# The first norm of a hybrid encoder block: loads, weight halves, scaling and two weight sums moved to other engines

## The chip, the core and the metric

The kernel runs on one core of a Trainium2 chip. The core has a matrix engine (TensorE, PE in the profile), a vector engine (VectorE, DVE), an activation engine (ScalarE, ACT), a general engine (GpSimd, POOL) and a sequencer that asks for transfers (SyncE, SP). Each runs its own list of instructions in order and waits on semaphores where it needs what another engine or a DMA has made. The metric is the device time of one execution in microseconds.

## The reference

Inputs are float32. The hidden state is 16 meta tokens followed by x, 1024 tokens of 1024 channels.

```python
def rmsnorm(x, g):
    y = xf * lax.rsqrt(jnp.mean(xf * xf, axis=-1, keepdims=True) + EPS)
    return (y * g).astype(x.dtype)

h = concat([meta, x])
u = rmsnorm(h, norm_mix)
z = u @ w_in                     # 4112 columns: a, q, k, v, r, lr, ga, gb
p = multiscale_pool(a)           # trailing means of 2, 4, 8, 16 tokens, minus the token
o = gla_chunked(q, k, v, log_sigmoid(lr @ w_gate_up + b_gate) / 16)
m = sigmoid(ga) * (p-branch) + sigmoid(gb) * (o-branch)
h = h + m @ w_out
h = h + square(relu(rmsnorm(h, norm_ffn) @ w_ff1)) @ w_ff2
out = rmsnorm(h, norm_final)[16:]
```

## The kernel before

Every matrix product is computed as three products of split operands (a high part, rounded to the matrix engine's fast 32-bit type, and a low part, the rest): high x high, low x high, high x low. ACT makes the high part, DVE subtracts it from the value to make the low part. After the norm come the gate, q and r columns of `w_in` (the class `Quarters`: a Strassen-like scheme of seven products P1 to P7 over pairs of weight blocks, each block first split into high and low), the pooling branch, the linear attention, the merge, and the MLP. The change touches the function `start`, which is the first 45 us or so, and what `Quarters` makes ready in it.

What `start` does:

- It asks for x's first tile of 128 tokens (`load(0)`, into the buffer `xs` of four tiles), the identity matrix, the norm weight (`g8`, in the first rows of the tile `xm`), x's second tile, two raw tiles of v weights (`fetch_vw`), and x's third and fourth tile, all on SP, in this order; POOL asks for the sixteen `lr` columns. The two raw tiles hold the v columns 0 to 127 and 128 to 255, each for all 1024 input rows.
- For each tile t of 128 tokens: `squared` (ACT squares it and sums each row), `root` (two small ACT instructions), `rest` (the inverse root, refined with three to five tiny instructions; on DVE for tiles 0 to 2, on POOL from tile 3 on, and for the meta tokens, tile 8), `normed` (DVE multiplies the tile by its inverse root into `us`, L664, SP then asks for tile t + 4, and PE transposes the result into two PSUM banks, L582), `taken` (DVE multiplies the transposed halves by the norm weight into `ut`, L589; ACT makes the high half `th`, L598; DVE the low half `tl`, L599).
- `warm(n)` lets PE transpose the identity into a bank that nobody reads, 4, 8 and 12 times (`WARM`), between the first real steps.
- `load_vw` splits the v weights: `hi` on ACT (L475), `lo` on DVE (L478), `lr` for the sixteen more columns. `v_tile` is the product of one tile of tokens with these 272 columns, eight k steps for each of the three parts. Tiles 0 and 1 run part by part ("hh", "lh", "hl", L510), tiles 2 to 7 step by step (L256 to L258). Two PSUM banks take them in turn, and ACT evacuates each into `v` (L525) and `lrtok` (L529).
- In the last turns of the loop `q.prime` splits the first weight blocks of `Quarters`. Its P5 operand is the sum of two halves of a weight block; DVE adds them (L325) into a half of the tile `fs`. `differences` then makes sums and differences of the `ut` quarters, on DVE, and steps through the first products (`next(run)`).

The order of the work around the change is written by hand: in `start` ACT, DVE and POOL run in program order (`manual_schedule`), and PE does so everywhere. SP's list follows the calls, and an SP request waits until the buffer that it fills is read out, with all later requests behind it.

```python
for t in range(1, 8):
    left_now, leave = leave, v_tile(0, t, True)   # t > 1
    if t < 6: b[t + 2] = normed(t + 2)
    for fn in left_now: fn()                      # evacuate tile t - 1
    if t < 6: rest(t + 3)
    lows = list(taken(b[t + 1], t + 1))
    if t < 5: squared(t + 4); root(t + 4)
    for fn in lows: fn()
    for n in {5: (0,), 6: (1, 2), 7: (3,)}.get(t, ()): q.prime(n == 0)
```

Of the kernel before, what the change touches and what calls it, by code (L numbers as in the profile page):

```python
# [33 lines left out]
WARM = (4, 8, 12)  # L34
# [80 lines left out]
def kernel(  # L115
# [173 lines left out]
    class Quarters:  # L289
# [4 lines left out]
        def __init__(self, n, block, places, result):  # L294
            self.n, self.block, self.places, self.result = n, block, places, result
            self.w, self.x, self.room = {}, {}, False
            self.leaving, self.lead = None, 0

        def load(self, i, u):
            dst = self.places[i % 2][u]  # L300
            self.w[i, u] = dst.rearrange("p (k c) -> p k c", k=KT)
            nc.sync.dma_start(self.w[i, u], self.block(2 * i + u))

# [11 lines left out]
        def sums(self):  # L315

            for p, i in self.order():
                a11, a12 = (self.w[i, 0][:, k : k + 4] for k in (0, 4))
                if p in ("P1", "P2"):
                    s = a11 if p == "P1" else a12  # L320
                else:
                    a21, a22 = (self.w[i, 1][:, k : k + 4] for k in (0, 4))
                    s = quad(S["fs"][:, i % 2] if p != "P7" else S["s3"])
                    if p == "P5":
                        dve.tensor_tensor(s, a21, a22, ALU.add)  # L325
                    elif p == "P6":
                        dve.tensor_tensor(s, s, a11, ALU.subtract)
                    elif p == "P7":
                        dve.tensor_tensor(s, a11, a21, ALU.subtract)
                    elif p == "P3":  # L330
                        dve.tensor_tensor(s, a12, s, ALU.subtract)
                    elif p == "P4":
                        s = a22
                yield p, i, s
# [132 lines left out]
    def fetch_vw(i):  # L467
        return [raw.load(w_cols(C_V + i * 256 + j * P), D).rearrange("p (k c) -> p k c", k=KT) for j in range(2)]

    def load_vw(i, raws=None, parts=False):  # L470
        vw, raws = S["vw"][i], raws or fetch_vw(i)
        c = [slice(j * P, (j + 1) * P) for j in range(2)]

        def hi(j):
            act.activation(vw[:, 0, :, c[j]], raws[j], ACT.Copy)  # L475

        def lo(j):
            dve.tensor_tensor(vw[:, 1, :, c[j]], raws[j], f32(vw[:, 0, :, c[j]]), ALU.subtract)  # L478
# [14 lines left out]
    def v_tile(i, t, later=False, by_part=False, by_k=False):  # L493
# [12 lines left out]
        def part(name):  # L506
            left_of["n"] -= 1
            l, r = parts[name]
            for k in range(KT):
                pe.matmul(b, l[:, k], r[:, k], start=name == "hh" and k == 0, stop=left_of["n"] == 0 and k == KT - 1)  # L510
# [115 lines left out]
    def start():  # L626
        act.preload_act_table_set("natural_log_exp_and_others")
# [22 lines left out]
        load(0)  # L650
        nc.sync.dma_start(ident, ident_in)
        nc.sync.dma_start(g8, norm_mix.rearrange("(k p) -> k p", p=P))
        load(1)
# [7 lines left out]
        def normed(t):  # L661

            x_, u = of(t)
            dve.tensor_scalar(u, x_, rs[t], None, ALU.mult)  # L664
# [3 lines left out]

        def warm(n):

            for _ in range(n):
                pe.transpose(idle[:, :P], ident, ident)
# [4 lines left out]
        with tc.manual_schedule(engines={mybir.EngineType.Activation, mybir.EngineType.DVE, mybir.EngineType.Pool}):  # L677
# [15 lines left out]
            warm(WARM[1])  # L693
            squared(0)
# [6 lines left out]
            lows = [list(taken(b[0], 0))]  # L701
            rest(1)
            warm(WARM[2])
            b[1] = normed(1)
            hi, lo, lr = load_vw(0, raws, True)
            hi(0)
            hi(1)
            lr_lo = lr()
            v0, leave0 = v_tile(0, 0, by_part=True)
            v1, leave = v_tile(0, 1, by_part=True)  # L710
            v0("hh")
# [3 lines left out]
            lows.append(list(taken(b[1], 1)))  # L715
            v1("hh")
            for j in range(2):
                lo(j)
            lr_lo()
# [15 lines left out]
            for t in range(1, 8):  # L735
# [17 lines left out]
                if t < 6:  # L753
                    rest(t + 3)
                lows = list(taken(b[t + 1], t + 1)) if t < 7 else []
# [1097 lines left out]
```

## Time and profile before

| what | value |
|---|---|
| three executions | 1212.27, 1213.29 and 4245.53 us; median 1213.29 |
| the profiled execution | 1212.85 us, of which the span from first to last instruction is 1211.0 |
| PE, DVE, ACT, POOL busy | 98%, 72%, 51%, 5% of the span |
| mean granted TensorE clock | 0.998 |
| bytes moved | 182 MB, mean 150 GB/s |

The profile shows one execution. Its rows give the start of an instruction or of a group in microseconds from the start of the span, its length, the engine, the line of the kernel, the operation and out<-in by the names of the tiles, and in brackets how long the engine had been idle before it and what ended that. Lengths of neighbours on an engine overlap a little, so the distance between two starts is the better price of a step in a sequence. A matmul row's end is modelled; a PE that shows no gap is taken as busy.

### The profile page before, as it was taken

Reading aid. Unit: us, or ns where it says so; the run is one execution under the profiler, and the core shown is the slowest. Engines: PE = TensorE matmul, PEld = TensorE weight load, DVE = VectorE, ACT = ScalarE, POOL = GpSimd, SP = SyncE. Lnnn points to the kernel's source line nnn. Section 1 sums busy time; section 2 is a strip of 40 time slices with the busy share of each in tenths; the row PEclk is TensorE's granted clock in tenths of the full one; section 3 lists DMA queues with packets and bytes.
Section 4 is the critical chain, followed back from the end, with each engine's and each line's share of the span. In section 5 each row is a group of like instructions: output and inputs, shape, how many; then the busy total and the mean of one; then the engine's idle time right before and its main releaser. Section 6 shows DMA issues by size and latency. Waiting matters only on the chain.

```text
span 1211.0 us, 18406 instructions
## 1 busy us (share of the span) xinstructions
PE 1191.4 (98%) x6794; PEld 992.8 (82%) x6794; DVE 874.3 (72%) x1442; ACT 623.3 (51%) x1115; POOL 60.3 (5%) x98
## 2 busy tenths in 40 slices
PE   7999999999999999999999999999999999999997
PEld 7878888898887877888878888888888888888886
DVE  7996677666667878636886767677675887887786
ACT  7667567744546423315655545455454444444554
POOL 2000000000103226000000000000000000000000
PEclk9999999999999999999999999999999999999999
DMA  9043433545107665922254444444479973333532
GB/s 256 2 113 114 121 94 102 154 125 159 40 20 258 196 206 196 327 89 88 87 158 164 152 143 156 146 161 149 153 251 322 348 226 97 98 99 92 174 96 87
DMA packets 144554, 182.24 MB, mean 150 GB/s; under 512 B 10264, under 2 KB 81712, under 8 KB 143952
## 3 DMA queue, kind: packets, MB, share of 16 engines
q1 hardware_dynamic: 143856, 176.81, 45.3%
q0 software_dynamic: 608, 4.26, 1.0%
q8 instruction: 53, 0.87, 0.3%
q14 instruction: 37, 0.30, 0.1%
HBM read 123.36 MB, written 57.67 MB: 149 GB/s over the span
## 4 chain that ended last, share of the span: by engine, by line
PE 87%; DVE 7%; ACT 3%; issue 1%; DMA 1%; POOL 0%; SPq 0%; DVEq 0%; ACTq 0%; POOLq 0%
PE b_mm L256 10%; PE b_mm L258 10%; PE b_mm L257 10%; PE b_ms L257 9%; PE b_ms L258 9%; PE b_ms L256 9%; PE b_x L257 8%; PE b_x L256 8%; PE b_x L258 8%; PE b_sc L1249 1%; PE b_mx L256 1%; PE b_mx L258 1%; PE b_mx L257 1%; DVE w1l L275 1%; DVE ut L787 1%
## 5 line engine op out<-in xcount | busy, mean ns | idle before, releaser
L256 PE MATMUL b_mm<-th,w1h 128*128 128x512 f32 (+1 forms) x308 | 116.2, 377 | 2.0 <-DVE c L822 1.0
L258 PE MATMUL b_mm<-th,w1l 128*128 128x512 f32 (+1 forms) x308 | 114.2, 371 | 0.0
L257 PE MATMUL b_mm<-tl,w1h 128*128 128x512 f32 (+1 forms) x308 | 114.2, 371 | 0.0
L256 PE MATMUL b_x<-th,w1h 128*128 128x512 f32 (+1 forms) x264 | 100.2, 379 | 0.0
L257 PE MATMUL b_x<-tl,w1h 128*128 128x512 f32 (+1 forms) x264 | 100.1, 379 | 0.0
L258 PE MATMUL b_x<-th,w1l 128*128 128x512 f32 (+1 forms) x264 | 99.7, 378 | 0.0
L274 ACT ACTIVATE w1h<-raw 128x512 fp32r<-128x512 f32 x98 | 60.7, 620 | 28.1 <-PE b_ms L257 13.6
L274 ACT ACTIVATE w1h<-fs 128x512 fp32r<-128x512 f32 x78 | 49.0, 630 | 48.1 <-PE b_ms L257 33.9
L275 DVE TENSOR_TENSOR w1l<-raw,w1h 128x512 fp32r<-128x512 f32 x98 | 67.0, 684 | 8.4 <-ACT w1h L274 8.4
L256 PEld LDWEIGHTS b_mm<-th,w1h 128*128 128x128 f32 x308 | 57.8, 188 | 13.6 <-issue 1.9
L258 PEld LDWEIGHTS b_mm<-th,w1l 128*128 128x128 f32 x308 | 57.9, 188 | 10.2
L257 PEld LDWEIGHTS b_mm<-tl,w1h 128*128 128x128 f32 x308 | 57.8, 188 | 9.3
L275 DVE TENSOR_TENSOR w1l<-fs,w1h 128x512 fp32r<-128x512 f32 x78 | 53.3, 686 | 16.3 <-ACT w1h L274 16.2
L274 ACT ACTIVATE w1h<-bt 128x512 fp32r<-128x512 f32 x44 | 27.8, 632 | 66.5 <-issue 62.2
L258 PEld LDWEIGHTS b_x<-th,w1l 128*128 128x128 f32 x264 | 49.7, 188 | 9.5
L256 PEld LDWEIGHTS b_x<-th,w1h 128*128 128x128 f32 x264 | 49.6, 188 | 9.5
L257 PEld LDWEIGHTS b_x<-tl,w1h 128*128 128x128 f32 x264 | 49.6, 188 | 9.2
L1701 DVE TENSOR_TENSOR bt<-w,w 128x512 f32<-128x512 f32 x80 | 54.7, 684 | 2.1 <-DMA w<-in_w_ff_dram 2.1
L274 ACT ACTIVATE fxh<-bt 128x512 fp32r<-128x512 f32 x36 | 22.8, 632 | 56.3 <-issue 50.6
L274 ACT ACTIVATE w1h<-rawx 128x512 fp32r<-128x512 f32 x44 | 27.5, 628 | 45.0 <-PE b_x L257 18.7
L258 PE MATMUL b_ms<-wo,w1l 128*128 128x512 f32 x128 | 49.9, 390 | 0.0
L256 PE MATMUL b_ms<-wo,w1h 128*128 128x512 f32 x128 | 49.8, 389 | 0.0
(447 smaller groups left out, 3331.8 us busy)
## 6 DMA issues: line engine op xcount, KB each, us to landing
hf_dram<-h SPq DMA_DIRECT2D x112, 256.0 KB, 2.1
raw<-hf_dram SPq DMA_DIRECT2D x112, 256.0 KB, 2.7
w<-in_w_ff_dram SPq DMA_DIRECT2D x64, 256.0 KB, 4.7
raw<-in_w_in_dram SPq DMA_DIRECT2D x22, 512.0 KB, 4.3
raw<-in_w_ff_dram SPq DMA_DIRECT2D x16, 512.0 KB, 4.2
rawx<-in_w_ff_dram SPq DMA_DIRECT2D x16, 512.0 KB, 4.1
rawx<-in_w_in_dram SPq DMA_DIRECT2D x10, 512.0 KB, 4.3
xs<-in_x_dram SPq DMA_DIRECT2D x8, 512.0 KB, 5.5
```

What stands on the lines that cost most here:

```text
L256: pe.matmul(ps, ah, bh, start=first and i == 0, stop=False, skip_group_check=more)
L257: pe.matmul(ps, ah, bl, start=False, stop=False, skip_group_check=more)
L258: pe.matmul(ps, al, bh, start=False, stop=last and i == n - 1, skip_group_check=more)
L274: act.activation(hi, a, ACT.Copy)
L275: dve.tensor_tensor(lo, a, f32(hi), ALU.subtract)
L787: dve.tensor_tensor(to_, a_, b_, ALU.subtract)
L1249: pe.matmul(b[to, e, j], kk[r, s], qq[r, s], start=True, stop=True, tile_position=(e * CH, u * CH))
L1701: dve.tensor_tensor(bt, w, S["w2"][q[3:]][:, i], ALU.add if q[2] == "+" else ALU.subtract)
```

## The change

- The first loads: x's second tile is asked for right after the first on SP; the norm weight is asked for by ACT instead of SP, and the load of ACT's function table comes after that request; the identity comes third on SP.
- The v weights come as row halves: a raw tile holds input rows 0 to 511 or 512 to 1023 for all 256 columns (the same for the second set of v weights, `load_vw(1)`). The `hi` and `lo` of a half cover four k steps, and tile 0's first part is written in two runs of four k steps.
- ACT's and DVE's order in the first 16 us is changed: the `lr` high part first, tile 0's `taken` between the two weight halves; on DVE `ut` of tile 0 after the scaling of tile 1.
- `warm` multiplies a zeroed block of `fs` by itself, 14, 3, 2 and 1 times, instead of transposing the identity.
- Tiles 3, 5 and 7 are scaled on ACT (an activation with a scale for each row) instead of DVE.
- The P5 sums of weight pairs 0 and 1 are made by four POOL transfers after POOL's last statistics: one that writes the first half into `fs`, and one that adds the second half to it.

```diff
-WARM = (4, 8, 12)
+WARM = (14, 3, 2, 1)
...
-            self.leaving, self.lead = None, 0
+            self.leaving, self.lead, self.summed = None, 0, set()
...
+        def load_sum(self, i):
+
+            s, w = quad(S["fs"][:, i % 2]), self.block(2 * i + 1)
+            self.summed.add(i)
+            pool.dma_start(s, w[:, :4])
+            pool.dma_start(s, w[:, 4:], accum_op=ALU.add)
...
                     if p == "P5":
-                        dve.tensor_tensor(s, a21, a22, ALU.add)
+                        if i not in self.summed:
+                            dve.tensor_tensor(s, a21, a22, ALU.add)
...
     def fetch_vw(i):
-        return [raw.load(w_cols(C_V + i * 256 + j * P), D).rearrange("p (k c) -> p k c", k=KT) for j in range(2)]
+        rows = lambda j: w_in[j * HALF : (j + 1) * HALF, C_V + i * 256 : C_V + (i + 1) * 256]
+        return [raw.load(rows(j).rearrange("(k p) c -> p k c", p=P), D).rearrange("p (k c) -> p k c", k=4) for j in range(2)]
...
-        c = [slice(j * P, (j + 1) * P) for j in range(2)]
+        at = lambda n, j: vw[:, n, 4 * j : 4 * j + 4, :256]
 
         def hi(j):
-            act.activation(vw[:, 0, :, c[j]], raws[j], ACT.Copy)
+            act.activation(at(0, j), raws[j], ACT.Copy)
 
         def lo(j):
-            dve.tensor_tensor(vw[:, 1, :, c[j]], raws[j], f32(vw[:, 0, :, c[j]]), ALU.subtract)
+            dve.tensor_tensor(at(1, j), raws[j], f32(at(0, j)), ALU.subtract)
...
-        def part(name):
-            left_of["n"] -= 1
+        def part(name, ks=range(KT)):
+            left_of["n"] -= ks[-1] == KT - 1
             l, r = parts[name]
-            for k in range(KT):
+            for k in ks:
...
     def start():
-        act.preload_act_table_set("natural_log_exp_and_others")
...
         load(0)
+        act.dma_start(g8, norm_mix.rearrange("(k p) -> k p", p=P))
+        load(1)
         nc.sync.dma_start(ident, ident_in)
-        nc.sync.dma_start(g8, norm_mix.rearrange("(k p) -> k p", p=P))
-        load(1)
+        act.preload_act_table_set("natural_log_exp_and_others")
         raws = fetch_vw(0)
...
             x_, u = of(t)
-            dve.tensor_scalar(u, x_, rs[t], None, ALU.mult)
+            if t in (3, 5, 7):
+                act.activation(u, x_, ACT.Copy, scale=rs[t])
+            else:
+                dve.tensor_scalar(u, x_, rs[t], None, ALU.mult)
...
+        blank = S["fs"][:, 0, :P]
+        dve.memset(blank, 0.0)
+
         def warm(n):
 
             for _ in range(n):
-                pe.transpose(idle[:, :P], ident, ident)
+                pe.matmul(idle[:, :P], blank, blank, start=True, stop=True)
...
             squared(1)
             root(1)
-            lows = [list(taken(b[0], 0))]
             rest(1)
             warm(WARM[2])
             b[1] = normed(1)
+            warm(WARM[3])
             hi, lo, lr = load_vw(0, raws, True)
+            lr_lo = lr()
             hi(0)
+            low = list(taken(b[0], 0))
             hi(1)
-            lr_lo = lr()
+            lows = [low, list(taken(b[1], 1))]
             v0, leave0 = v_tile(0, 0, by_part=True)
             v1, leave = v_tile(0, 1, by_part=True)
-            v0("hh")
+            v0("hh", top)
+            v0("hh", end)
             for fn in lows[0]:
                 fn()
             v0("lh")
-            lows.append(list(taken(b[1], 1)))
             v1("hh")
+            lr_lo()
             for j in range(2):
                 lo(j)
-            lr_lo()
             v0("hl")
...
+                if t == 5:
+                    q.load_sum(0)
+                    q.load_sum(1)
```

Three places of the order, of before and of the change. A row gives the line, the operation, and out<-in with the tiles' numbers; line numbers of the change are some ten higher.

ACT from the square of tile 1 to th of tile 1, before (`us<-xs` is a square, `raw0`, `raw1` the weight tiles, `ut00`, `ut01` the two halves of a transposed tile):

```order
L610 ACTIVATE us_167,small_99<-xs_163 128x1024
L612 ACTIVATE small_99<-small_99 128x1
L613 ACTIVATE small_99<-small_99 128x1
L598 ACTIVATE th0_132<-ut00_211 128x4x128
L598 ACTIVATE th0_132<-ut01_199 128x4x128
L475 ACTIVATE vw0_215<-raw0_116 128x8x128
L475 ACTIVATE vw0_215<-raw1_120 128x8x128
L482 ACTIVATE vw0_215<-lrraw_159 128x8x16
L598 ACTIVATE th0_132<-ut00_211 128x4x128
L598 ACTIVATE th0_132<-ut01_199 128x4x128
```

The same place with the change:

```order
L619 ACTIVATE us_166,small_99<-xs_162 128x1024
L621 ACTIVATE small_99<-small_99 128x1
L622 ACTIVATE small_99<-small_99 128x1
L491 ACTIVATE vw0_214<-lrraw_158 128x8x16
L484 ACTIVATE vw0_214<-raw0_116 128x4x256
L607 ACTIVATE th0_132<-ut00_210 128x4x128
L607 ACTIVATE th0_132<-ut01_198 128x4x128
L484 ACTIVATE vw0_214<-raw1_120 128x4x256
L607 ACTIVATE th0_132<-ut00_210 128x4x128
L607 ACTIVATE th0_132<-ut01_198 128x4x128
```

Tile 0's th has moved behind the first weight half, and the lr columns ahead of it.

DVE in the same stretch, before, from the norm weight's copy to the weights' low parts:

```order
L698 COPY small_99<-b_ms_232 128x8
L589 TENSOR_TENSOR ut00_211<-b_ms_250,small_99 128x4x128
L589 TENSOR_TENSOR ut01_199<-b_ms_251,small_99 128x4x128
L615 TENSOR_SCALAR small_99<-small_99 128x1
L617 SCALAR_TENSOR_TENSOR small_99<-small_99 128x1
L618 SCALAR_TENSOR_TENSOR small_99<-small_99 128x1
L664 TENSOR_SCALAR us_167<-xs_163,small_99 128x1024
L599 TENSOR_TENSOR tl0_136<-ut00_211,th0_132 128x4x128
L599 TENSOR_TENSOR tl0_136<-ut01_199,th0_132 128x4x128
L589 TENSOR_TENSOR ut00_211<-b_ms_285,small_99 128x4x128
L589 TENSOR_TENSOR ut01_199<-b_ms_286,small_99 128x4x128
L478 TENSOR_TENSOR vw0_215<-raw0_116,vw0_215 128x8x128
```

And with the change:

```order
L714 COPY small_99<-b_ms_243 128x8
L624 TENSOR_SCALAR small_99<-small_99 128x1
L626 SCALAR_TENSOR_TENSOR small_99<-small_99 128x1
L627 SCALAR_TENSOR_TENSOR small_99<-small_99 128x1
L676 TENSOR_SCALAR us_166<-xs_162,small_99 128x1024
L598 TENSOR_TENSOR ut00_210<-b_ms_256,small_99 128x4x128
L598 TENSOR_TENSOR ut01_198<-b_ms_257,small_99 128x4x128
L598 TENSOR_TENSOR ut00_210<-b_ms_277,small_99 128x4x128
L598 TENSOR_TENSOR ut01_198<-b_ms_278,small_99 128x4x128
L608 TENSOR_TENSOR tl0_136<-ut00_210,th0_132 128x4x128
L608 TENSOR_TENSOR tl0_136<-ut01_198,th0_132 128x4x128
L492 TENSOR_TENSOR vw0_214<-lrraw_158,vw0_214 128x8x16
```

Tile 0's ut has moved behind the scaling of tile 1, and its tl behind the ut of both tiles.

ACT at the scaling of tile 3, before, from the square of tile 4 to th of tile 2:

```order
L610 ACTIVATE us_167,small_99<-xs_163 128x1024
L612 ACTIVATE small_99<-small_99 128x1
L613 ACTIVATE small_99<-small_99 128x1
L525 ACTIVATE v0_148<-b_mm_298 128x256
L529 ACTIVATE lrtok_155<-b_mm_298 128x16
L598 ACTIVATE th0_132<-ut00_211 128x4x128
L598 ACTIVATE th0_132<-ut01_199 128x4x128
```

And with the change:

```order
L619 ACTIVATE us_166,small_99<-xs_162 128x1024
L621 ACTIVATE small_99<-small_99 128x1
L622 ACTIVATE small_99<-small_99 128x1
L674 ACTIVATE us_166<-xs_162,small_99 128x1024
L534 ACTIVATE v0_148<-b_mm_299 128x256
L538 ACTIVATE lrtok_154<-b_mm_299 128x16
L607 ACTIVATE th0_132<-ut00_210 128x4x128
L607 ACTIVATE th0_132<-ut01_198 128x4x128
```

The scaling, L674, stands ahead of tile 0's evacuation and of tile 2's th. POOL's end of the stage, before:

```order
L615 TENSOR_SCALAR small_99<-small_99 16x1
L620 TENSOR_TENSOR small_99<-small_99 16x1
L621 TENSOR_TENSOR small_99<-small_99 16x1
L622 TENSOR_SCALAR small_99<-small_99 16x1
L623 TENSOR_TENSOR small_99<-small_99 16x1
L773 CAST mask_91<-mf_175 128x384
```

And with the change:

```order
L632 TENSOR_TENSOR small_99<-small_99 16x1
L308 DMA fs_182<-in_w_in_dram 128x4x128
L309 DMA fs_182<-in_w_in_dram 128x4x128
L308 DMA fs_182<-in_w_in_dram 128x4x128
L309 DMA fs_182<-in_w_in_dram 128x4x128
L794 CAST mask_91<-mf_174 128x384
```

The four transfers stand between the last statistics and the mask; each L309 waits on POOL for the L308 ahead of it.

More of the change, by code (lines that the diff above doesn't have):

```diff
@@ L693, in start @@
             warm(WARM[1])
+            top, end = range(4), range(4, KT)
             squared(0)
```

## The prediction

> **What bounds the kernel.** I read the page first (PE busy for 98% of the span), then the busy time by stretch, the waits, the chain, and last the timeline of the first 75 us, one engine at a time. Busy time in four stretches, columns in the order span, PE, PEld, DVE, ACT, POOL, clock, DMA, GB/s, and below it the largest PE wait that comes after the first stretch:
>
> ```profile
> 0.00:22.16 22.16, 15.50 (x107) 13.92 (x107) 13.87 (x30) 15.34 (x33) 5.15 (x17) 1.00 0.93 274
> 22.16:37.30 15.14, 15.14 (x124) 15.14 (x125) 13.92 (x22) 13.20 (x35) 4.85 (x22) 1.00 0.46 113
> 37.30:74.44 37.14, 36.11 (x202) 29.91 (x200) 35.70 (x47) 22.88 (x42) 0.00 (x0) 1.00 0.13 35
> 74.44:1211.00 1136.56, 1124.65 (x6364) 933.80 (x6364) 810.79 (x1344) 571.86 (x1007) 50.26 (x59) 1.00 0.47 152
> ...
> PE b_mm L256 <- DVE c L822: 1.0, 1, 1.0
> ```
>
> TensorE idles 6.66 us before 22.16, nothing from there to 37.30, and 1.03 us in the third stretch, all of it in one wait for VectorE. The rest of its idle time lies behind 74.44, where the instruction streams stay the same. So the change can take back at most 6.66 + 1.03 = 7.7 us, 0.6% of the span, and only by starting TensorE's unbroken run earlier or by removing that one wait. Where PE has no gap, faster transfers and freed engines buy nothing.
>
> The start, engine by engine (start, length, engine, line, out<-in, and what ended the idle time before it); the last line is from the view of the raw weight tiles, the first of which is asked for at 2.45:
>
> ```profile
> 0.74 0.38 SPq L649 DMA_DIRECT2D xs<-in_x_dram  x1
> 2.05 0.35 SPq L649 DMA_DIRECT2D xs<-in_x_dram  x1
> 4.56 1.06 ACT L610 ACTIVATE us<-xs 128x1024 f32<-128x1024 f32 x1 [2.54 <-DMA xs<-in_x_dram]
> 7.76 1.06 ACT L610 ACTIVATE us<-xs 128x1024 f32<-128x1024 f32 x1 [1.43 <-DMA xs<-in_x_dram]
> 8.59 1.29 DVE L589 TENSOR_TENSOR ut<-b_ms,small 128x512 f32<-128x512 f32 x2 [0.95 <-PE b_ms L582]
> 10.45 1.99 ACT L475 ACTIVATE vw<-raw 128x1024 fp32r<-128x1024 f32 x2
> 10.51 0.75 DVE L664 TENSOR_SCALAR us<-xs,small 128x1024 f32<-128x1024 f32 x1
> 11.17 1.28 DVE L599 TENSOR_TENSOR tl<-ut,th 128x512 fp32r<-128x512 f32 x2
> 13.09 1.23 ACT L598 ACTIVATE th<-ut 128x512 fp32r<-128x512 f32 x2 [0.46 <-DVE ut L589]
> 13.58 2.35 DVE L478 TENSOR_TENSOR vw<-raw,vw 128x1024 fp32r<-128x1024 f32 x2
> 14.23 1.05 ACT L610 ACTIVATE us<-xs 128x1024 f32<-128x1024 f32 x1
> 15.83 1.04 ACT L610 ACTIVATE us<-xs 128x1024 f32<-128x1024 f32 x1
> 16.75 0.75 DVE L664 TENSOR_SCALAR us<-xs,small 128x1024 f32<-128x1024 f32 x1
> 17.06 0.49 POOL L615 TENSOR_SCALAR small<-small 128x1 f32<-128x1 f32 x1 [14.36 <-ACT us L610]
> 17.66 0.48 POOL L620 TENSOR_TENSOR small<-small 128x1 f32<-128x1 f32 x1
> 19.14 0.19 POOL L623 TENSOR_TENSOR small<-small 128x1 f32<-128x1 f32 x1
> 19.37 0.75 DVE L664 TENSOR_SCALAR us<-xs,small 128x1024 f32<-128x1024 f32 x1 [0.67 <-POOL small L623]
> 20.25 0.19 POOL L620 TENSOR_TENSOR small<-small 128x1 f32<-128x1 f32 x1
> 20.75 1.23 ACT L598 ACTIVATE th<-ut 128x512 fp32r<-128x512 f32 x2 [1.28 <-DVE ut L589]
> 22.16 0.39 PE L258 MATMUL b_mm<-vw,tl 128*128 128x272 f32 x1 [0.21 <-DVE tl L599]
> ...
> DMA to landing us min/median/max: 6.3/7.3/8.3
> ```
>
> Read it backwards: the run starts at 22.16 because tile 2's low part was late; that waited for th (20.75), ut, the scaling of tile 3 on DVE (19.37), POOL's statistics of tile 3 (17.06 to 19.33), its squares on ACT (15.83), and, in front of all that, x's second tile (7.76). Starts on one engine give the cost of a step in sequence: a square with its root 15.83 - 14.23 = 1.60, a th pair 1.14, one weight half 1.0 on ACT and 1.13 on DVE, a pair of ut or tl on DVE 1.2.
>
> **Part 1, the start.** x's second tile is issued second instead of fourth, some 0.9 us earlier, and no longer behind ident and the norm weight. The first tile went from issue at 0.74 to use at 4.56, 3.8 us; the second took 5.7. Issued at about 1.15 it lands between 4.95 and 6.85. ACT needs its 1.6 us for the first tile, to 6.2. I take 6.35, since it must move behind the first tile's 512 KB: 1.4 us earlier than 7.76. DVE then finishes tile 1's statistics and starts its scaling 10.51 - 7.76 = 2.75 us after the square, less the 0.5 us it stood behind ut: 8.6. New order on DVE: scaling 0.66, ut of tiles 0 and 1 2.4, tl 1.2, the three weight subtractions 2.5, statistics 0.7, so tile 2 is scaled at 16.05 instead of 16.75.
>
> On ACT the weights now come as row halves. The first is asked for 0.4 us earlier, and by the 6.3 to 8.3 us of the raw tiles lands between 8.35 and 10.35; the same bytes stand ahead of it, so I take the median, 9.35, less a little for rows of 1 KB: 9.2. From there 1.0, th 1.14, 1.0, th 1.14 give 13.5 for the square of tile 2 (was 14.23), and 15.1 for that of tile 3. POOL starts tile 3's five statistics 17.06 - 15.83 = 1.23 us after that square, at 16.3, and takes 2.27 us (17.06 to 19.33) under the same DVE work: 18.6. Now ACT, not DVE, scales tile 3, some 0.95 us (a square's 1.05 less the overlap with the next instruction): 19.55. Queued behind that on ACT are tile 0's two evacuations (0.45, by the rows of part 2), then th of tile 2: 20.0. Its first half is there at 20.65, DVE's low part 0.65 later: 21.3 against 22.16. This part gives 0.9 us. The 1.4 us at the head are not all kept, because the weights (9.2) and the scaling in ACT's queue are late next.
>
> Bounds of it: if the tile lands no earlier than before, DVE's new order scales tile 2 at 17.45, 0.7 later than now, which takes back what ACT gains: 0. If POOL runs at the 0.19 us of its row at 20.25, POOL gains another 1 us, but ACT is busy with two more squares until 15.1 + 2 x 1.6 = 18.3: 1.2, and about 1.5 with earlier weights. I take 0.9, where each queue is filled by its own rows.
>
> The warm-up costs nothing: PE does nothing useful before the first tile is scaled at 7.5, and the fourteen products need no transfer. If the clock fell back before 7.5, the eight transposes might take twice the 0.87 us of a row in part 2, to 9.3, and ut, now behind the second scaling at 9.3, covers that. The table load and the norm weight's issue share ACT's 4 us ahead of 4.56.
>
> **Part 2, tiles 3 to 7.** The transposes that open each tile on PE, from the chain, then ACT's cycle (evacuation, th, the next evacuation):
>
> ```profile
> 25.17 0.87 PE b_ms L582 x8
> 29.04 0.87 PE b_ms L582 x8
> ...
> 23.55 0.37 ACT L525 ACTIVATE v<-b_mm 128x256 f32<-128x256 f32 x1
> 24.01 1.23 ACT L598 ACTIVATE th<-ut 128x512 fp32r<-128x512 f32 x2
> 26.81 0.37 ACT L525 ACTIVATE v<-b_mm 128x256 f32<-128x256 f32 x1
> ```
>
> PE needs 3.9 us a tile, ACT 3.26. Scaling on ACT makes that 4.2 on every second tile, 3.74 on average: under 3.9. It is tightest at tile 4: th starts at 20.0 + 3.26 + 4.2 = 27.45, its low part is there 1.3 later, at 28.75, and PE wants it at 21.3 + 2 x 3.9 = 29.1. 0.35 us are in hand. DVE loses 0.75 us three times where PE sets the pace. Worth nothing, and costs nothing.
>
> **Part 3, the two sums.** VectorE's backlog from 37.3 on ends in the wait at 74.44:
>
> ```profile
> 41.79 0.67 DVE L325 TENSOR_TENSOR fs<-raw 128x512 f32<-128x512 f32 x1
> 53.89 0.68 DVE L325 TENSOR_TENSOR fs<-raw 128x512 f32<-128x512 f32 x1
> 54.61 0.63 ACT L274 ACTIVATE w1h<-fs 128x512 fp32r<-128x512 f32 x1 [0.25 <-DVE fs L325]
> 73.61 0.68 DVE L822 TENSOR_TENSOR c<-b_mm,u3p 128x512 f32<-128x512 f32 x1
> ```
>
> Each sum takes 0.60 off DVE. The first is whole; of the second ACT's queue takes some 0.45 back, as its copy at 54.61 stands behind an evacuation paced by PE. 0.75 to 1.2 us, capped by the 1.03 us of the wait: I take 0.85. In their place POOL issues four transfers, each sum's second half held until the first has landed; the mask and a memset queue behind, whose reader on ACT comes after its copy of the second sum. The nearest rows (the last column is us to landing):
>
> ```profile
> 34.37 0.18 POOL L623 TENSOR_TENSOR small<-small 16x1 f32<-16x1 f32 x1
> 1.29 1.07 POOL L655 DMA_DIRECT2D lrraw<-in_w_in_dram  x1 [0.46 <-issue]
> lrraw<-in_w_in_dram POOLq DMA_DIRECT2D x1, 64.0 KB, 5.1
> raw<-hf_dram SPq DMA_DIRECT2D x112, 256.0 KB, 2.7
> th<-pm_dram POOLq DMA_DIRECT2D x2, 1024.0 KB, 7.7
> ```
>
> POOL is free at about 34.4. With L from issue to landing the second sum stands at 34.4 + 1.07 + 3 L, and ACT wants it at 54.61 - 0.9 = 53.7. L = 2.7, the same size, gives 43.6; L = 5.1, the same queue, 50.8; an adding transfer that took twice 5.1 would give 55.9. I take L = 4 (same size, slower queue), 47.5: hidden. The point at which it isn't is L = 6.1.
>
> The Trainium skill, DMA: Bandwidth & Descriptors, section Anatomy of one DMA, gives 2.0 us plus the bytes over 436 GB/s for a transfer from this queue. By that, L is an estimated 2.6 us and the second sum stands at 43.3; for the megabyte it is 4.4, where the row has 7.7, so the row decides, and the late sums stay a rival. The sum of the terms is the same by both.
>
> **The sum.** 0.9 + 0 + 0.85 = 1.75 us. The profiled execution took 1212.85 around its span of 1211.0; its time becomes 1211.1. It lies 0.4 below the median shown (1213.29) and 0.6 above the lowest (1212.27), so it can stand for them.
>
> **Rivals.**
>
> Slower: the sums come late. For it: the POOL queue's 7.7 us, and POOL's 0.48 while DVE subtracts from two tiles in SBUF (17.66), 0.19 while it reads PSUM (20.25). From 37 to 74 DVE mostly does the former. With L = 7.7 the second sum lands at 58.6, 4.9 late; ACT and DVE behind it slide, the wait at 74.44 becomes 1.0 + 4.9 - 1.2 = 4.7, and the time 1212.85 - 0.9 + 3.7 = 1215.65. It decides from L = 6.1 on, and costs more than all gains from about 6.7. Against it: 7.7 is for four times the bytes. The Trainium skill, GPSIMD Engine Reference, section Specifications, says that GpSimd shares its SBUF interfaces with VectorE and contends with instructions of two SBUF inputs; by that rule the trace agrees, 0.48 against 0.19.
>
> No gain at the start: x's tile lands late, or ScalarE, with 0.35 us in hand, becomes the bound of tiles 3 to 7 (with 0.3 us more for each of three scalings 0.9 - 0.35 = 0.55 is lost). Start 0 to 0.35, sums 0.85: about 1211.8.
>
> More at the start: POOL runs free of DVE and the weights come at once, 1.5 + 1.03: 1210.3.
>
> The change does nothing at all, as PE is 98% busy: 1212.8. Against it stand the 6.66 and 1.03 us of idle PE.
>
> **Chances.** My forecast, 1210.6 to 1211.7: 0.5. No gain at the start, up to 1212.4: 0.2. More at the start, down to 1209.7: 0.12. Nothing: 0.08. Late sums, 1213 to 1216: 0.1. Leaving out the late sums and the tail of the good case, and with the half microsecond by which runs lie apart, the range is 1209.6 to 1213.4. All of these lie within 2%, about what a measurement of this kernel can tell from no change, which is 24 us: faster 0.01, same 0.97, slower 0.02 for a cost that no row here shows.
>
> **What would show it.** Right: the first unbroken PE row near 21.3; the square of x's second tile near 6.4; DVE's scaling of tile 2 near 16; PE's wait at the evacuation (now some 73) under 0.3 us; ACT's copies of fs with no wait for a DMA. Wrong: a PE wait for low parts between 21 and 36, ACT's copy of fs ended by a DMA, or a second tile landing past 7.

## The result, and the profile after

The change takes 1210.55 us (median of 22 runs, 1210.13 to 1212.15) against 1212.70 us for the kernel before on the same chip: a ratio of 0.9983, 95% interval 0.9977 to 0.9990. The 2.15 us are far inside the 2% that count as no change, but the interval lies clear of 1; it stands for a gain of 1.2 to 2.8 us. The execution of 4245.53 us shown above is left out of the ratio. The forecast was 1211.1. The profiled execution took 1210.59 us around a span of 1208.8, where before it was 1212.85 around 1211.0.

The busy time by stretch, cut at the same places of the program as in the prediction (first unbroken product, PE's second stretch, end of the evacuation wait), in the same columns, and PE's waits for the evacuation and in the MLP stage:

```profile
0.00:20.99 20.99, 17.60 (x123) 16.08 (x124) 13.15 (x30) 16.35 (x34) 4.39 (x17) 1.00 0.90 287
20.99:36.00 15.01, 15.01 (x123) 15.01 (x124) 11.57 (x19) 14.31 (x36) 5.12 (x21) 1.00 0.52 119
36.00:72.80 36.80, 36.25 (x203) 30.03 (x201) 35.57 (x47) 22.91 (x44) 3.96 (x5) 1.00 0.29 63
72.80:1208.80 1136.00, 1124.54 (x6364) 933.89 (x6364) 810.90 (x1344) 571.80 (x1007) 50.24 (x59) 1.00 0.47 152
...
PE b_mm L256 <- DVE c L843: 0.6, 1, 0.6
PE b_mm L256 <- DVE h L1660: 0.2, 1, 0.2
```

The run starts 1.17 us earlier (22.16 to 20.99). The second stretch is as tight as before, PE busy for 15.01 of 15.01. The third is 0.34 shorter between rounded cuts; by the rows, the product behind the evacuation stands at 72.82 instead of 74.44. So 1.62 us are gained by then, of which 0.45 is the wait for `c`, 1.03 before and 0.57 now. The remaining 0.6 us between the two spans lie behind 72.8, where the instruction streams are the same; the last experiment looks at them.

The start on the engines, in the form of the prediction's rows (start, length, engine, line, out<-in, idle time and what ended it):

```profile
1.05 4.74 PE L687 MATMUL b_x<-fs 128*128 128x128 f32 x28 [1.05 <-DVE metab L1234]
6.24 1.04 ACT L619 ACTIVATE us<-xs 128x1024 f32<-128x1024 f32 x1
6.35 0.20 PE L707 MATMUL b_ms<-ident,xm 8*128 8x8 f32 x1 [0.56 <-DMA ident<-in_ident_dram]
7.62 1.09 PE L591 MATMUL b_ms<-ident,us 128*128 128x128 f32 x8 [0.21 <-DVE us L676]
8.29 1.06 ACT L484 ACTIVATE vw<-raw 128x1024 fp32r<-128x1024 f32 x1 [0.16 <-DMA raw<-in_w_in_dram]
9.08 2.48 DVE L598 TENSOR_TENSOR ut<-b_ms,small 128x512 f32<-128x512 f32 x4
9.80 1.23 ACT L607 ACTIVATE th<-ut 128x512 fp32r<-128x512 f32 x2 [0.45 <-DVE ut L598]
12.93 1.04 ACT L619 ACTIVATE us<-xs 128x1024 f32<-128x1024 f32 x1
15.76 0.19 POOL L624 TENSOR_SCALAR small<-small 128x1 f32<-128x1 f32 x1 [13.09 <-ACT us L619]
15.85 0.75 DVE L676 TENSOR_SCALAR us<-xs,small 128x1024 f32<-128x1024 f32 x1
17.97 0.19 POOL L632 TENSOR_TENSOR small<-small 128x1 f32<-128x1 f32 x1
18.20 1.15 ACT L674 ACTIVATE us<-xs,small 128x1024 f32<-128x1024 f32 x1 [0.37 <-POOL small L632]
19.58 1.15 ACT L607 ACTIVATE th<-ut 128x512 fp32r<-128x512 f32 x2
20.99 0.40 PE L258 MATMUL b_mm<-vw,tl 128*128 128x272 f32 x1
```

x's second tile is squared at 6.24, and no bracket stands at that row: the tile was there before ACT had finished the first. The weight half is taken at 8.29, not 9.2. From there the chain of the prediction can be followed row by row: squares of tile 2 at 12.93, POOL's statistics of tile 3 from 15.76 to 18.16, the scaling on ACT at 18.20, th of tile 2 at 19.58, the run at 20.99. In front of the scaling ACT waits 0.37 us for POOL; in front of the first th it waits 0.45 us for DVE.

The evacuation's side, one row of before (the `ut` of tile 7), then the rows of after, with the landing times of the four transfers into `fs` as the last line:

```profile
37.32 1.29 DVE L589 TENSOR_TENSOR ut<-b_ms,small 128x512 f32<-128x512 f32 x2 [0.57 <-PE b_ms L582]
```

```profile
33.06 1.14 ACT L674 ACTIVATE us<-xs,small 128x1024 f32<-128x1024 f32 x1
34.36 0.86 POOL L308 DMA_DIRECT2D fs<-in_w_in_dram  x1
34.43 1.14 ACT L607 ACTIVATE th<-ut 128x512 fp32r<-128x512 f32 x2
35.07 1.29 DVE L608 TENSOR_TENSOR tl<-ut,th 128x512 fp32r<-128x512 f32 x2 [1.53 <-ACT th L607]
36.89 1.29 DVE L598 TENSOR_TENSOR ut<-b_ms,small 128x512 f32<-128x512 f32 x2
43.98 1.29 POOL L309 DMA_DIRECT2D fs<-in_w_in_dram  x1 [3.83 <-DMA fs<-in_w_in_dram]
53.10 0.61 ACT L274 ACTIVATE w1h<-fs 128x512 fp32r<-128x512 f32 x1
71.99 0.68 DVE L843 TENSOR_TENSOR c<-b_mm,u3p 128x512 f32<-128x512 f32 x1
...
DMA to landing us min/median/max: 3.4/4.9/4.9
```

Read the two `ut` rows of tile 7 together. Before, DVE had waited 0.57 us for PE's transposes there: it kept PE's pace. With PE 1.17 earlier the row should stand at 36.15. It stands at 36.89, and DVE has not waited for anything in front of it: DVE comes 0.74 late, because its tl of tile 6 at 35.07 had waited 1.53 for th, and th stood on ACT behind the scaling of tile 7 (33.06). So DVE enters its backlog 0.43 us earlier, not 1.17. Then it leaves out two sums of 0.60, and `c` stands at 71.99 instead of 73.61: 0.43 + 0.60 + 0.60 = 1.63. PE arrives 1.17 earlier, so its wait falls by 1.62 - 1.17 = 0.45. The second sum's last transfer was asked for at 43.98 and landed 4.9 later, at 48.9, where ACT copies it at 53.10 without a wait.

### The profile page after: what moved, and what is told of

Its sections match the earlier page's. It is cut to its first block, busy times and chain, and to the rows that moved or that the text cites. A ratio compares the mean times of both kernels' runs of the same rounds, so it can differ in the third digit from the quotient of the medians.

```text
span 1208.8 us, 18443 instructions
## 1 busy us (share of the span) xinstructions
PE 1193.4 (99%) x6810; PEld 995.0 (82%) x6810; DVE 871.2 (72%) x1438; ACT 625.4 (52%) x1118; POOL 63.7 (5%) x102
## 4 chain that ended last, share of the span: by engine, by line
PE 90%; DVE 6%; ACT 2%; issue 1%; DMA 1%; DVEq 0%; ACTq 0%
PE b_mm L256 10%; PE b_mm L258 10%; PE b_mm L257 10%; PE b_ms L257 9%; PE b_ms L256 9%; PE b_ms L258 9%; PE b_x L257 8%; PE b_x L256 8%; PE b_x L258 8%; PE b_sc L1270 1%; PE b_mx L256 1%; PE b_mx L258 1%; PE b_mx L257 1%; PE b_ms L591 0%; PE b_ms L1546 0%
## 5 line engine op out<-in xcount | busy, mean ns | idle before, releaser
L258 PE MATMUL b_mm<-th,w1l 128*128 128x512 f32 (+1 forms) x308 | 114.2, 371 | 0.0
L258 PE MATMUL b_x<-th,w1l 128*128 128x512 f32 (+1 forms) x264 | 99.7, 378 | 0.0
L258 PEld LDWEIGHTS b_mm<-th,w1l 128*128 128x128 f32 x308 | 57.9, 188 | 10.1
L258 PEld LDWEIGHTS b_x<-th,w1l 128*128 128x128 f32 x264 | 49.7, 188 | 9.5
L258 PE MATMUL b_ms<-wo,w1l 128*128 128x512 f32 x128 | 49.9, 390 | 0.0
```

The costliest lines, as they stand in the source:

```text
L258: pe.matmul(ps, al, bh, start=False, stop=last and i == n - 1, skip_group_check=more)
```

## The experiments

The theory: the start's gain hangs on x's second tile and the new order together, the sums each give DVE's 0.60 us to the evacuation, and the scaling on ACT takes part of that back. The rivals stand in each expectation. All times are medians of 11 runs (22 for the change and for before in the first rows), each beside the kernel before on the same chip (1212.55 to 1212.88). The run start is the start of tile 2's first product with a low part (L258); it and the wait are read from the one profiled execution of each version.

| version | us | ratio, 95% interval | run start | wait for `c` |
|---|---|---|---|---|
| before | 1212.70 | 1 | 22.16 | 1.0 |
| the change | 1210.55 | 0.9983 [0.9977, 0.9990] | 20.99 | 0.6 |
| e6, change with the old loads | 1212.40 | 0.9998 [0.9989, 1.0006] | 22.57 | 0.6 |
| e5, before with the new loads | 1214.20 | 1.0014 [1.0005, 1.0023] | 24.42 | 1.0 |
| e8, change with the old warm-up | 1212.62 | 1.0000 [0.9991, 1.0008] | 23.53 | none |
| e10, before with new loads and warm-up | 1211.96 | 0.9996 [0.9987, 1.0004] | 22.39 | 1.0 |
| e7, change with column halves | 1210.52 | 0.9984 [0.9975, 0.9993] | 21.09 | 0.6 |
| e2, change, all scaling on DVE | 1210.27 | 0.9981 [0.9972, 0.9990] | 21.04 | none |
| e3, change, only tile 3 on ACT | 1210.07 | 0.9979 [0.9970, 0.9988] | 21.05 | none |
| e11, e3 with tile 0 evacuated first | 1209.80 | 0.9976 [0.9967, 0.9985] | 20.81 | none |
| e1, change with the sums on DVE | 1211.56 | 0.9992 [0.9983, 1.0000] | 21.03 | 1.1 |
| e4, before with the sums by DMA | 1211.49 | 0.9991 [0.9982, 0.9999] | 22.38 | none |
| e9, change with a late second sum | 1214.92 | 1.0021 [1.0012, 1.0030] | 20.92 | none |
| e12, the change again | 1210.57 | 0.9981 [0.9972, 0.9990] | 20.97 | 0.6 |

**e6: what the early tile is worth.** The change with the order of loads of before.

```diff
+        act.preload_act_table_set("natural_log_exp_and_others")
...
         load(0)
-        act.dma_start(g8, norm_mix.rearrange("(k p) -> k p", p=P))
-        load(1)
         nc.sync.dma_start(ident, ident_in)
-        act.preload_act_table_set("natural_log_exp_and_others")
+        nc.sync.dma_start(g8, norm_mix.rearrange("(k p) -> k p", p=P))
+        load(1)
```

> The change with the first loads in their old order (identity and norm weight ahead of x's second tile, all from SP). Theory: ScalarE squares the second tile near 7.7 instead of 6.24, VectorE scales tile 2 near 17.3 instead of 15.85, and PE's unbroken run starts about 1 us later than 20.99, near 22: about 1211.5. Rival (weights and POOL set the start, not this tile): the run starts at 21.2 or before, 1210.6.

```profile
7.80 1.06 ACT L619 ACTIVATE us<-xs 128x1024 f32<-128x1024 f32 x1 [1.46 <-DMA xs<-in_x_dram]
17.43 0.75 DVE L676 TENSOR_SCALAR us<-xs,small 128x1024 f32<-128x1024 f32 x1
22.57 0.39 PE L258 MATMUL b_mm<-vw,tl 128*128 128x272 f32 x1
```

The square is 1.56 us later than in the change, the scaling of tile 2 1.58, the run 1.58, the time 1.85, more than was expected (a run at 22, 1211.5). With the change's order, everything behind it in the start moves with this tile one to one. The prediction's bound for a late tile forecast the scaling well (17.45) but called the start's gain 0; the run starts 0.41 us later than before.

**e5: the loads alone.** The kernel before with the change's order of loads, the same lines the other way round.

> The kernel before with nothing but the order of the first loads changed (x's second tile second, norm weight from ScalarE, identity third). Theory (the second tile gains only where VectorE's order lets it through; before, its statistics stand behind ut of tile 0, which waits for PE until 8.59): ScalarE squares the second tile near 6.3 instead of 7.76, but VectorE's scaling of it stays near 10.5 and PE's unbroken run starts within 0.2 us of 22.16, about 1212.6. Rival (the load alone is the cause): the run starts near 21 and the time falls by 1 us.

PE's rows to tile 0's transposes (L582), and DVE's first row behind them:

```profile
6.46 1.12 PE L672 MATMUL b_x<-ident 128*128 128x128 f32 x4 [6.46 <-DMA ident<-in_ident_dram]
7.71 1.97 PE L672 MATMUL b_x<-ident 128*128 128x128 f32 x8
9.47 1.91 PE L582 MATMUL b_ms<-ident,us 128*128 128x128 f32 x8
10.57 0.69 DVE L589 TENSOR_TENSOR ut<-b_ms,small 128x512 f32<-128x512 f32 x1 [2.58 <-PE b_ms L582]
```

A miss: slower than before by 1.55 us. The identity, now third in the queue, lands at 6.46 (before at 4.77), and twelve warm-up transposes that read it stand on PE ahead of tile 0's. Those come at 9.47 instead of 7.77, and at the slow spacing: 1.91 us where the change's take 1.09. The run starts 2.26 us later. What was won for one tile was taken by the transfer that it overtook.

**e8: the change with the old warm-up.**

```diff
-WARM = (14, 3, 2, 1)
+WARM = (4, 8, 12, 0)
...
-                pe.matmul(idle[:, :P], blank, blank, start=True, stop=True)
+                pe.transpose(idle[:, :P], ident, ident)
```

> The change with the old warm-up, transposes of the identity (4, 8, 12). Theory (the identity now lands after x's second tile, at 6.35, and twelve transposes and the norm weight stand ahead of tile 0 on PE): tile 0's transposes begin near 9 instead of 7.62, ut of tile 0 about 0.9 us later, PE's unbroken run 0.5 to 0.9 us later: about 1211.2. Rival (nothing waits for PE before 10 us): no change, 1210.55.

```profile
9.54 1.66 PE L591 MATMUL b_ms<-ident,us 128*128 128x128 f32 x8
10.64 1.29 DVE L598 TENSOR_TENSOR ut<-b_ms,small 128x512 f32<-128x512 f32 x2 [1.20 <-PE b_ms L591]
```

The same 9.5 as in e5, and here it costs the whole gain: the run starts 2.54 later than in the change, the time is 2.07 longer, three times what was expected. Tile 0's transposes start 1.92 us later and take 0.57 longer (1.66 for 1.09), which is nearly all of the 2.54. The warm-up on a zeroed block is no ornament. It keeps PE's list free of anything that waits for the identity until the identity is needed.

**e10: loads and warm-up, without the new order on ACT and DVE.** e5 with the zeroed block and `WARM` of the change.

> The kernel before with the change's order of first loads and its warm-up on a zeroed block, and nothing else: ACT's and DVE's order, the weight halves, the scaling and the sums as before. Theory (loads and warm-up belong together and bring most of the start; the order on ACT and DVE the rest): tile 0's transposes stand at 7.6 again, not at 9.5 as with the loads alone, x's second tile is squared at 6.3, tile 2 scaled near 16.1, run start near 21.5 (-0.7), PE's wait at the evacuation 1.0 still, time about 1212.0. Rival (the new order of DVE and ACT is what turns the early tile into an early run): ut of tile 0 and tl keep DVE from the scaling of tile 1, tile 2 is scaled at 16.6 or later, run start 22.0 to 22.2, time 1212.5.

```profile
1.05 6.28 PE L675 MATMUL b_x<-fs 128*128 128x128 f32 x28 [1.05 <-DVE metab L1217]
6.30 1.04 ACT L610 ACTIVATE us<-xs 128x1024 f32<-128x1024 f32 x1
8.18 1.04 PE L582 MATMUL b_ms<-ident,us 128*128 128x128 f32 x8
8.82 1.29 DVE L589 TENSOR_TENSOR ut<-b_ms,small 128x512 f32<-128x512 f32 x2 [1.12 <-PE b_ms L582]
10.73 0.75 DVE L664 TENSOR_SCALAR us<-xs,small 128x1024 f32<-128x1024 f32 x1
```

By the rows the rival is nearer, though its run start of 22.0 to 22.2 is missed too. The tile is squared at 6.30, as in the change, but DVE stands 1.12 us idle before `ut` of tile 0, with the statistics of tile 1 behind it in its list; tile 1 is scaled at 10.73, not earlier than before (10.51). The run starts at 22.39, 0.23 later than before, just as far as `ut` of tile 0 (8.82 against 8.59). The time, 1211.96, is what the theory expected (1212.0), but its interval takes in 1.

Two things keep the 0.23 from being a price. Runs of the same code differ by as much: e4 has the start of before, unaltered, and its run starts at 22.38. And the execution that was profiled had a slow blank block, 6.28 us where the change's took 4.74 and 5.42, so tile 0's transposes stand at 8.18. Had they stood at 7.62, as in the change, the run would start near 21.8 (an estimate, 22.39 - 0.56), still 0.8 later than in the change. So most of the 1.17 us needs the new order, and by this estimate the loads with the warm-up alone would bring some 0.3. Each of e5, e6, e8 and e10 lacks one or two of the three edits, and none of their profiles has a run that starts earlier than before's.

**e7: column halves instead of row halves** of the v weights, as before.

```diff
-        return [raw.load(rows(j).rearrange("(k p) c -> p k c", p=P), D).rearrange("p (k c) -> p k c", k=4) for j in range(2)]
+        return [raw.load(w_cols(C_V + i * 256 + j * P), D).rearrange("p (k c) -> p k c", k=KT) for j in range(2)]
...
-            v0("hh", top)
-            v0("hh", end)
+            v0("hh")
```

> The change with the v weights as column halves, as before (rows of 512 bytes; the first product waits for both halves). Theory (the row halves land earlier, ScalarE took the first at 8.29 where 9.2 was reckoned): the first half is taken 0.5 to 1 us later, tile 3's square and with it POOL and PE's unbroken run some 0.3 to 0.6 us later: about 1210.9 to 1211.2. Rival (the halves are covered): the run starts at 20.99, 1210.55.

The first half is taken at 8.61 instead of 8.29 (8.42 in e12, which is the change again) and the run starts at 21.09 instead of 20.99 (20.97). Time and interval are those of the change, and the run is nearer to the rival's 20.99 than to the 21.3 to 21.6 expected: the row halves are worth some 0.1 us by the rows, and nothing that the time shows.

**e2 and e3: scaling on ACT.** e2 scales no tile on ACT; e3 scales only tile 3 there (`t == 3`).

```diff
-            if t in (3, 5, 7):
+            if t in ():
```

> The change, but tiles 3, 5 and 7 scaled on VectorE as before. Theory (ScalarE's scaling of tiles 5 and 7 makes th late, VectorE stood idle 1.53 us for it at 35.07, and so its backlog begins 0.74 us too late): VectorE's ut of tile 7 starts near 36.1 instead of 36.89, PE's wait for the evacuation c falls from 0.6 to 0, the time to about 1210.0; PE's unbroken run still starts near 21.0. Rival (the scaling on ScalarE is what starts PE's run earlier): the run starts 0.5 us or more later, 1211 or above.

> The change, but only tile 3 scaled on ScalarE, 5 and 7 on VectorE. Theory: PE's unbroken run starts at 20.99 as in the change, VectorE's ut of tile 7 near 36.1, PE's wait for c 0, about 1210.0. Rival (scaling on ScalarE relieves VectorE): VectorE is later and the wait grows beyond 0.6, 1211.

From e3's trace, the `ut` of tile 7 and the evacuation:

```profile
36.19 1.29 DVE L598 TENSOR_TENSOR ut<-b_ms,small 128x512 f32<-128x512 f32 x2 [0.61 <-PE b_ms L591]
71.59 0.68 DVE L843 TENSOR_TENSOR c<-b_mm,u3p 128x512 f32<-128x512 f32 x1
```

In both the run starts where it does with the change (21.04, 21.05), so the scaling on ACT brings nothing at the start. And in both the `ut` of tile 7 stands where PE's shift puts it (36.20 and 36.19, ended by PE again), `c` is 0.4 us earlier, and PE's wait for it is gone. Scaling tiles 5 and 7 on ACT cost the change this 0.4. It is less than the 0.7 us at the `ut` of tile 7, as DVE then waits longer for ACT: in e3 0.66 us at 45.21 and 0.19 at 53.78, where the change has 0.48 and none. By time alone, 1210.27 and 1210.07 against 1210.55, intervals overlap; the rows are what shows it.

**e11: ACT's idle 0.37 us filled.** e3, and tile 0's evacuations ahead of the scaling of tile 3.

```diff
                 else:
-                    left_now = leave0
+                    left_now = ()
+                    for fn in leave0:
+                        fn()
                 if t < 6:
                     b[t + 2] = normed(t + 2)
```

> The change with only tile 3 scaled on ACT, and tile 0's two evacuations ahead of that scaling on ACT, in the time in which ACT stands idle for POOL's statistics of tile 3 (0.37 us before the scaling at 18.20), instead of behind it. Theory (ACT's chain scaling, evacuations, th of tile 2 sets the run's start): th of tile 2 starts some 0.35 earlier, run start about 20.65 instead of 20.99, no wait at the evacuation, time about 1209.75 against 1210.07 for the version with tile 3 alone. Rival (POOL or DVE's ut of tile 2 sets it): run start 20.9 or later, time 1210.1.

```profile
18.22 1.15 ACT L674 ACTIVATE us<-xs,small 128x1024 f32<-128x1024 f32 x1
19.27 1.14 ACT L607 ACTIVATE th<-ut 128x512 fp32r<-128x512 f32 x2
19.69 1.04 PE L591 MATMUL b_ms<-ident,us 128*128 128x128 f32 x8
20.81 0.28 PE L258 MATMUL b_mm<-vw,tl 128*128 128x272 f32 x1
```

The lowest median, 1209.80, though its interval overlaps those of e3, e2 and the change. th of tile 2 comes 0.31 us earlier than in the change, the run 0.18 instead of 0.35 (0.24 earlier than in e3): PE's own transposes of tile 3, still at 19.7 behind the scaling, now set the end. Ahead of the scaling ACT's evacuation and POOL's last statistic of tile 3 now end together, both at 18.2, so by the rows neither alone would bring more.

**e1 and e4: the sums.** e1 is the change without them, e4 the kernel before with them alone.

```diff
-                if t == 5:
-                    q.load_sum(0)
-                    q.load_sum(1)
```

> The change, but both P5 sums back on VectorE. Theory (VectorE's backlog up to 73 us is what PE waits for, and each sum is 0.60 us of it): the evacuation c comes 1.2 us later, PE's wait for it grows from 0.6 to about 1.8 us, the time from 1210.55 to about 1211.7. Rival (PE is the bound there and the sums were covered anyway): 1210.5, the wait stays at 0.6.

> The kernel before with nothing but the two sums moved to POOL's transfers. Theory: VectorE's backlog is 1.2 us shorter, PE's wait of 1.03 us at 74.44 is gone, 1212.7 becomes about 1211.7; PE's unbroken run starts at 22.16 as before. Rival (transfers beside the work cost what they save, or arrive late): 1212.7 or more, with ScalarE's copies of fs ended by a transfer.

From e1's trace:

```profile
73.19 0.68 DVE L840 TENSOR_TENSOR c<-b_mm,u3p 128x512 f32<-128x512 f32 x1
...
PE b_mm L256 <- DVE c L840: 1.1, 1, 1.1
PE b_ms L258 <- DVE w1l L275: 0.3, 1, 0.3
```

`c` stands 1.20 us later than in the change: two sums of 0.60, the second whole too. PE loses 1.19 by then, in the wait for `c` and in shorter ones for w1l ahead of it (1.8 had been expected in the wait for `c` alone), and the time is 1.01 longer. e4 is 1.13 shorter than its runs of before, with the wait of 1.03 gone; from the run's start to the product behind the evacuation PE needs 51.39 us instead of 52.28. Its run starts at 22.38, 0.22 later than before's, with the same code: x's second tile was squared at 8.17, not 7.76. So the term is measured both ways, and the start of one kernel differs by 0.2 us between executions.

**e9: the slower rival, forced.** The second sum's two transfers are issued twice, so the same sum stands later.

```diff
                     q.load_sum(1)
+                    q.load_sum(1)
```

> The change with the second sum made twice over on POOL's queue, so that it stands late: with the legs as measured in the change (1.3 us of issue and 3.4 to 4.9 us to landing each) the second sum stands at about 48.9 + 10 = 58.8 instead of 48.9, where ACT's copy of it stood at 53.10 in the change, 5.7 late. Theory (the prediction's slower rival is a real mechanism: ACT and DVE behind the copy slide, and DVE's backlog hands it to the evacuation): ACT's copy of fs is ended by a DMA, PE's wait for DVE's evacuation grows from 0.6 to about 5 to 6 us, time about 1215.5, slower than the change by some 5. Rival (PE uses the second P5 operand late, and ACT and DVE make the lateness good before the evacuation): wait under 2, time under 1212.

```profile
52.93 1.28 POOL L309 DMA_DIRECT2D fs<-in_w_in_dram  x1 [2.85 <-DMA fs<-in_w_in_dram]
57.69 0.63 ACT L274 ACTIVATE w1h<-fs 128x512 fp32r<-128x512 f32 x1 [4.57 <-DMA fs<-in_w_in_dram]
76.18 0.68 DVE L844 TENSOR_TENSOR c<-b_mm,u3p 128x512 f32<-128x512 f32 x1
...
PE b_ms L258 <- DVE w1l L275: 1.8, 1, 1.8
PE b_ms L256 <- ACT w1h L274: 1.3, 1, 1.3
```

ACT's copy comes 4.59 us late and `c` 4.19; PE's product behind the evacuation stands at 77.06, 4.24 later than in the change, and the time is 4.37 longer. The price of a late sum is one to one, as the prediction had it; the place is not. PE does not wait for `c` at all. It waits 3.11 us in front of it, for the split weights of P4 (w1h, w1l) that stand behind the sum on ACT and DVE; the change idles 0.57 up to the same product. The other 1.70 is slower work: behind these waits the granted clock reads 0.50 from 73 to 76, and the products of P4 stand 0.43 us apart instead of 0.23. By the rows that adds little to the price, since the product stands 0.88 behind the start of `c` here and 0.83 in the change, where it does wait for it. The change has 53.10 - 48.9 = 4.2 us in hand against a late sum.

**e12: the change again**, unaltered, for the 0.6 us behind 72.8.

> The change itself once more, unaltered. In the profiles so far PE's one wait for h in the MLP stage is 0.8 us before, 0.2 in the change, and between none and 0.8 in the other versions, without following any edit. Theory (it is a matter of the single execution): in this profile of the same kernel it differs from 0.2 by more than 0.1, or the stretches behind 74 us differ by some tenths otherwise, while run start (20.99) and the wait at the evacuation (0.6) come out the same within 0.1. Rival (it belongs to the build, so that the change gains 0.6 us there): 0.2 again, and the span within 0.1 of 1208.8. Time in both 1210.5.

Run start and the wait for `c` come out the same, and the wait for `h` in the MLP stage, 0.2 us in the first profile, is not among the waits of this one (the least listed is 0.2). In the other versions it is 0.2, 0.4, 0.6, 0.7, 0.8 or absent. So it belongs to the single execution. Yet the two profiles end within 0.2 us of each other (spans 1208.8 and 1208.6), so the wait alone doesn't set the time behind 72.8.

From the product behind the evacuation to the end of the span it is 1136.0 us in the change and 1135.8 here. Over all fourteen profiles it is 1135.5 (e3) to 1136.6 (before), and it does not follow the edits: e4, e5 and e10, which are before with some of the edits, have 1135.8 to 1136.1. So the 0.6 us is no more than single executions differ by in this stretch, and the profile of before happens to be the longest. The gain that the rows show, 1.62, lies inside the interval of the measured one, 1.2 to 2.8. Whether there is a rest to explain stays open.

## Why the prediction came out, point by point

**Part 1, the start: mechanism right, size 0.9 for 1.17.** The tile was squared at 6.24 (6.35), tile 2 scaled at 15.85 (16.05). The mis-sized term is the first weight half, 8.29 instead of 9.2. The raw tiles' median of 7.3 us was applied to a transfer that started earlier, and it landed after 6.2, just below their lower end. Of these 0.9 us 0.3 reach the run, since ACT then waits 0.45 us for `ut` and 0.37 for POOL, whose statistics took 2.40 us (2.27). The rival of more at the start had the weights' half of its condition, and POOL's not. The shape of the halves, which e7 was to show as the cause of the early landing, is at most a small part of it: column halves are taken at 8.61, also well ahead of 9.2, and start the run at 21.09.

**The warm-up: its cost was right, its role was missed.** "The warm-up costs nothing" holds. But the prediction weighed it as a cost only, and did not ask who else waits for the identity that was moved behind x's second tile. e5 and e8 give the answer: tile 0's transposes at 9.5, and a run that starts 2.3 us later than before and 2.5 later than in the change.

**Part 2, the step that failed: "Worth nothing, and costs nothing."** It was checked against PE alone, and PE does keep its pace (15.01 of 15.01 us). But DVE follows ACT's th, the scaling of tile 7 makes DVE 0.74 late at its next step, and from there DVE is what PE waits for. The 0.35 us in hand were counted for the engine that had no wait ahead of it. So the sign "wait under 0.3 us" did not come; it is 0.57, and gone in e2 and e3, which are 0.4 us ahead of the change at `c`.

**Part 3, the sums: the second was worth 0.60, not 0.15.** By e1 `c` moves by the whole 1.20, so what ACT's queue holds back was not on DVE's path to the evacuation. L was 3.4 us once and 4.9 three times for the 4 taken, and the second sum stood at 48.9 for 47.5. The rival of the late sums had the right price and did not occur. The Trainium skill, DMA: Bandwidth & Descriptors, section Anatomy of one DMA, gives an estimated 2.6 us for 256 KB on this path; the trace shows 3.4 for a plain transfer that runs alone and 4.9 for the others, so the measurement decides, as it did for the megabyte.

**The sum.** Forecast 0.9 + 0 + 0.85 = 1.75; measured up to 72.8 us 1.17 + 0.45 = 1.62, the 0.45 being 1.20 from the sums, less 0.74 for the scaling. Three errors nearly cancel: more at the start, more from the sums, a cost in part 2. That the total came so near is luck in this sense. The time, 1210.55, is half a microsecond lower than forecast and falls just below the band of the forecast (from 1210.6), in that of more at the start; by the rows, which give 1.62, this is not more gain at the start but the stretch behind 72.8, where single executions differ by as much.

## What to carry to other kernels

When a transfer is moved forward, ask who waits for those that it overtakes, on every engine's list: here the early tile paid only with a warm-up that needs no transfer and an order on DVE that doesn't stand behind the late one. When work moves to an engine "with time in hand", follow its results into the engine that will be late next, not only into the one that is busy now. When times differ by some tenths of a microsecond in a thousand, read the rows of the stage (a start, a wait that is gone) beside the medians, in more than one profile, and account for the gain stretch by stretch: here the start of one kernel differed by 0.2 us between executions, and a right total hid errors that cancel.

## What the hardware showed that was not expected

The same fourteen blank products (28 rows) took 4.74 us in the change, 5.42 when it ran again, and 6.28 in e10. They start at 1.05 in each; at 6.28 / 28 = 0.22 us a row e10 runs the whole block at the slow spacing, while in the change (0.17 on average) a faster spacing begins within it. The granted clock reads 1.00 in every stretch of the start, so this shows only in the rows' spacing; in e9, by contrast, the profile does show a clock of 0.50 after PE had idled 3.1 of 3.9 us. The Trainium skill, TensorE: Matmul & The Clock Gate, Part 1, puts the change of spacing some 4 us into sustained work, give or take 0.5; e10's block shows it later than that. In the change it costs nothing, as tile 0's transposes stand at 7.62 and 7.61 both times; in e10 they stood at 8.18.

A transfer that adds to what is in SBUF took longer than a plain one of the same 256 KB where each ran alone: 4.9 us against 3.4 in the change, 4.8 against 3.4 in e4, 4.7 to 4.9 against 3.3 to 3.6 in e9. The plain one that was issued right behind an adding one took 4.9 to 5.0 us as well.
